# One step of a hybrid decoder on one core: x read by quarters of its rows and transposed on VectorE, with w_in read in the order that this gives

## The chip, the core and the metric

The kernel runs on one core of a Trainium2 chip. Its engines are TensorE (PE in the profile; its weight loads are PEld), VectorE (DVE), ScalarE (ACT), GpSimd (POOL) and SyncE (SP); the last mostly issues transfers, which 16 DMA engines carry out. The metric is the device time of one execution in microseconds (us). Three runs of the kernel before took 2526.93, 2530.73 and 2531.6 us; their median, 2530.73 us, is the time before. The time of the changed kernel is the median of its runs.

## What is computed

One decoder layer for two groups with the same weights: a prompt of 256 tokens and 8 samples of 4 tokens, so 288 tokens of width 2048. All values are 32-bit floats.

```python
def _layer(x, mem_k, mem_v, ssd_conv, ssd_state, gla_state, ffn_conv, p):
    xn = _rmsnorm(x, p['norm_mix'])
    z, xbc, dt_raw, q, k, v, r, g_lr, gate_a, gate_b = _split(xn @ p['w_in'], IN_SIZES)
...
    merged = sigmoid(gate_a) * branch_a + sigmoid(gate_b) * branch_b
    h = x + merged @ p['w_mix_out']
    h = h + _cross_attend(_rmsnorm(h, p['norm_cross']), mem_k, mem_v, p['w_cq'], p['w_co'])
...
```

Ahead of it stand the keys and values of the memory for the prompt, `mn @ w_ck` and `mn @ w_cv` with mn the normalised memory (256 rows). w_in is 2048 x 15408. The sum over the 2048 elements of a token in `xn @ w_in` may be taken in any order, if x and w_in are read in the same one. That freedom is what the change uses.

## The kernel before, in words

**Layout.** Activations stand transposed: features on the 128 partitions, 16 k-tiles of 128 features, and the 288 tokens along the free axis. A projection (`proj`, L158, and `proj_w`, L132) loads a block of four k-tiles by 256 columns of a weight (512 KB, tile `raw`, three buffers) over SP's queue. `wsplit` (L100) cuts each pair of k-tiles into a rounded high part `whi` (ACT, L103) and the rest `wlo` (DVE, L105), five buffers each. TensorE then takes three products per k-tile and 128 columns: high weight by high and by low activation (L147, L148), and low weight by high activation (L151). The next weight block is issued on SP when `wlo` has read the buffer that it takes.

**The first stage.** `mem_proj` (L293) makes the memory's keys and values, eight heads' worth, each in 16 k-steps of six matmuls with 512 columns (L315, L316, L319). It reads w_ck and w_cv by 256 KB per k-step. The first of the eight also prepares the memory rows (tile `mt`, two times 128 rows of 2048 elements). Between the k-steps of the next four, two generators are woven in by `weave` (L172): `x_norm` into heads two and three (L474), `x_prep` into heads four and five (L475).

**x_norm** (L385) loads x by nine transfers of 256 KB over SP's queue: `x_load(0)` brings the 32 sample tokens into `xs`, the other eight a quarter of the columns of 128 prompt rows each into `xp`, which takes the buffer of `mt`. Tokens are on partitions. ACT squares 512 columns at a time with a running sum (L391, twelve instructions, since the 32 sample tokens take four of their own), DVE adds the sums up, ACT takes Ln and Exp of a 128 x 3 tile, which gives each token's 1/rms. Three DVE instructions (L428) put these on diagonals, one TensorE product with ones (L431) spreads them to all partitions, and DVE copies the result to `rtok` (L432).

**x_prep** (L436) runs over the 16 k-tiles. For each, TensorE transposes three 128 x 128 blocks into PSUM (L442, tile `mm`, three buffers), ACT copies the 128 x 288 result to `xf` (L445), every second time SP stores `xf` to the DRAM tensor `x_d` (L447), DVE multiplies the PSUM tile by `rtok` (L449), and `split_from` (L183) multiplies by the gain `norm_mix` and cuts into the high part (ACT, L184) and the low part (DVE, L185). These are the two halves `X(k)` of the activations of every w_in product. The gain comes from `vcol`, a transposed table of the small vectors (`names`, L88).

**Later.** w_in is read by `proj` for all its parts but dt and the gate ranks, which `dt_load` (L486) reads in 32 and 16 columns. `load_x` (L1317) reads `x_d` back over POOL's queue, two k-tiles a transfer, three transfers ahead, for the residual sum at L1337.

**Order.** A scheduler with a model of the engines orders the instructions of each engine when the program is built. The first head of `mem_proj` is ordered by hand, and the nine loads of x keep their order among each other.

Of the kernel before, what the change touches and what calls it, by code (L numbers as in the profile page):

```python
# [8 lines left out]
F32 = mybir.dt.float32  # L9
# [7 lines left out]
P = 128  # L17
D = 2048
# [24 lines left out]
def hybrid_step(ctx: ExitStack, tc: tile.TileContext, I: dict, O: list):  # L43
# [38 lines left out]
    for q in (2, 3):  # L82
# [2 lines left out]

    vcol = const.tile([P, 116], F32, name="vcol")
    scw = const.tile([P, 96], F32, name="scw")
    names = [("norm_mem", 16), ("norm_mix", 16), ("ssd_norm", 16), ("norm_cross", 16), ("norm_ffn", 16),  # L88
             ("b_gla_gate", 8), ("gla_norm", 4), ("ssd_conv_b", 24)]
    vofs = {}  # L90
    dcol = const.tile([P, KT], F32, name="dcol")
# [3 lines left out]
    def vec(name):  # L95
        o, n = vofs[name]
        return vcol[:, o:o + n]
# [34 lines left out]
    def proj_w(load, ncol, X, nk, cons, N=T):  # L132
# [126 lines left out]
    ma_d = dram.tile([P, KT, T], F32, name="ma_d")  # L259
    mg_d = dram.tile([P, KT, T], F32, name="mg_d")  # L260
    ga_d = dram.tile([P, KT // 2, T], F32, name="ga_d")
    x_d = dram.tile([P, KT, T], F32, name="x_d")
    h_d = dram.tile([P, KT, T], F32, name="h_d")

    X = halves(bigr, "xn")
    with pool("p0") as p0:
# [7 lines left out]
        mt = p0.tile([P, 2, D], F32, tag="rows", name="mt")  # L274

        def mem_load(k0):
            cs = slice(k0 * P, (k0 + 2) * P)
# [81 lines left out]
        xts = [xp[:, 0, :], xp[:, 1, :], xs]  # L359
# [15 lines left out]

        def x_load(n):

            if n == 0:
                d = nc.sync.dma_start(out=xs[0:NS], in_=I["x_sample"].rearrange("b l d -> (b l) d"))
            else:  # L380
                i, cs = (n - 1) // 4, slice((n - 1) % 4 * 512, (n - 1) % 4 * 512 + 512)
                d = nc.sync.dma_start(out=xp[:, i, cs], in_=I["x_prompt"][0, i * P:(i + 1) * P, cs])
            tc.keep_in_program_order(d)

        def x_norm():  # L385
            sp4 = p0.tile([P, 3, 4], F32, name="sp4")
            ss = p0.tile([P, 3], F32, name="ss")

            def square(i, q):
                junk = p0.tile([P, 512], F32, name="junk")  # L390
                S.activation(junk, xts[i][:, q * 512:(q + 1) * 512], ACT.Square, accum_out=sp4[:, i, q:q + 1])  # L391

            for step in range(23):
                if step % 2 and step < 18:
                    x_load(step // 2)
                if step == 3:

                    V.tensor_reduce(mrs, mss, AX.X, ALU.add)
                    S.activation(mrs, mrs, ACT.Ln, scale=1.0 / D, bias=epsc[:, 0:1])
                    S.activation(mrs, mrs, ACT.Exp, scale=-0.5)  # L400
                if step == 6:
                    held.pop()()
                if step > 6 and step % 2 == 0 and step < 15:
                    square(2, step // 2 - 4)
                if step > 6 and step % 2:
                    square((step - 7) // 8, (step - 7) // 2 % 4)
# [24 lines left out]
            MM(a[:, 0:T], ones, dg.rearrange("p c t -> p (c t)")[:, 0:T], start=True, stop=True)  # L431
            V.tensor_copy(rtok, a[:, 0:T])  # L432

        rtok = p0.tile([P, T], F32, name="rtok")

        def x_prep():  # L436

            gx = vec("norm_mix")
            for k in range(KT):
                a = mm_tile()  # L440
                for i, xt in enumerate(xts):
                    TR(a[:, i * P:(i + 1) * P], xt[:, k * P:(k + 1) * P], ident)  # L442
                if k % 2 == 0:
                    xf = p0.tile([P, 2, T], F32, tag="xf", bufs=3, name="xf")
                S.copy(xf[:, k % 2, :], a[:, 0:T])  # L445
# [3 lines left out]
                V.tensor_tensor(xr, a[:, 0:T], rtok, ALU.mult)  # L449
# [36 lines left out]
        def dt_load(k0, kn):  # L486
            raw = wp.tile([P, kn, 112], F32, tag="raw", bufs=RB, name="raw")
            for o, c0, n in ((0, O_DT, 32), (32, O_G, 16)):
                nc.sync.dma_start(out=raw[:, :, o:o + n],
                                  in_=I["w_in"][k0 * P:(k0 + kn) * P, c0:c0 + n].rearrange("(k p) n -> p k n", p=P))  # L490
# [1324 lines left out]
```

## Time and profile before

| what | value |
|---|---|
| median of three runs | 2530.73 us (2526.93 to 2531.6) |
| the profiled execution | 2530.86 us, its span 2529.1 us |
| busy, share of the span | PE 99%, PEld 96%, DVE 69%, ACT 53%, POOL 16% |
| moved | 521.96 MB, mean 206 GB/s |
| w_in | 240 loads of 512 KB, and eight small ones |

The profile shows one execution, times in microseconds from the start of its span. A group of instructions is named by its line, engine, operation and the tiles that it writes and reads; "x" is the count, and the last numbers are busy time and the mean of one in nanoseconds. Idle time stands with what ended it ("<-"). In the table by stretches of time each engine has its busy time, then come TensorE's granted clock as a share of full speed, the busy share of the 16 DMA engines and the rate moved.

A matmul's duration in the profile runs from its start through the pipeline, and successive ones overlap. What one takes of TensorE's time is read from the starts of two neighbours, not from its duration.

### The profile page before, as it was taken

Reading aid. Unit: us, or ns where it says so; the run is one execution under the profiler, and the core shown is the slowest. Engines: PE = TensorE matmul, PEld = TensorE weight load, DVE = VectorE, ACT = ScalarE, POOL = GpSimd, SP = SyncE. Lnnn points to the kernel's source line nnn. Section 1 sums busy time; section 2 is a strip of 40 time slices with the busy share of each in tenths; the row PEclk is TensorE's granted clock in tenths of the full one; section 3 lists DMA queues with packets and bytes.
Section 4 is the critical chain, followed back from the end, with each engine's and each line's share of the span. In section 5 each row is a group of like instructions: output and inputs, shape, how many; then the busy total and the mean of one; then the engine's idle time right before and its main releaser. Section 6 shows DMA issues by size and latency. Waiting matters only on the chain.

```text
span 2529.1 us, 50509 instructions
## 1 busy us (share of the span) xinstructions
PE 2508.4 (99%) x18962; PEld 2418.5 (96%) x18962; DVE 1747.9 (69%) x3744; ACT 1342.7 (53%) x2724; POOL 392.2 (16%) x729
## 2 busy tenths in 40 slices
PE   9999999999999999999999999999999999999998
PEld 8889999998999999999999998999999999999998
DVE  6656777786867656667666577667777677675765
ACT  7655647655463645454454554555555455454545
POOL 3002133342300000000001022402111001020010
PEclk9999999999999999999999999999999999999999
DMA  8766587767868676767777699655555555555553
GB/s 268 220 218 196 169 252 206 229 197 209 236 188 271 184 241 185 242 202 265 205 223 249 199 327 322 211 164 173 169 173 170 170 172 172 167 172 171 169 170 130
DMA packets 442022, 521.96 MB, mean 206 GB/s; under 512 B 26876, under 2 KB 390236, under 8 KB 441712
## 3 DMA queue, kind: packets, MB, share of 16 engines
q1 hardware_dynamic: 407728, 422.34, 54.3%
q0 software_dynamic: 34016, 96.38, 12.0%
q8 instruction: 149, 2.44, 0.4%
q14 instruction: 97, 0.79, 0.1%
q10 hardware_dynamic: 32, 0.01, 0.0%
HBM read 473.13 MB, written 45.48 MB: 205 GB/s over the span
## 4 chain that ended last, share of the span: by engine, by line
PE 96%; DMA 2%; DVE 1%; POOL 1%; ACT 0%; issue 0%; DVEq 0%; ACTq 0%
PE acc L148 27%; PE acc L147 27%; PE acc L151 27%; PE acc L315 2%; PE acc L316 2%; PE acc L319 2%; DMA sqr<-in_state_ssd_dram 1%; PE la L1526 1%; PE la L1468 1%; PE mm L1147 1%; PE la L1138 1%; PE mm L1111 1%; POOL sqr L727 0%; DMA raw<-in_w_gla_out_dram 0%; DMA raw<-in_w_in_dram 0%
## 5 line engine op out<-in xcount | busy, mean ns | idle before, releaser
L103 ACT CAST whi<-raw 128x512 fp32r<-128x512 f32 x1464 | 895.1, 618 | 1016.0 <-PE acc L148 753.2
L105 DVE TENSOR_TENSOR wlo<-raw,whi 128x512 fp32r<-128x512 f32 x1464 | 994.4, 686 | 621.5 <-ACT whi L103 607.9
L147 PE MATMUL acc<-xn,whi 128*128 128x288 f32 (+1 forms) x1936 | 550.5, 299 | 0.0
L148 PE MATMUL acc<-xn,whi 128*128 128x288 f32 (+1 forms) x1936 | 542.3, 296 | 0.0
L151 PE MATMUL acc<-xn,wlo 128*128 128x288 f32 (+1 forms) x1936 | 414.1, 295 | 0.0
L148 PE MATMUL acc<-hf,whi 128*128 128x288 f32 x1408 | 393.2, 295 | 0.0
L147 PE MATMUL acc<-hf,whi 128*128 128x288 f32 x1408 | 389.0, 292 | 0.0
L147 PEld LDWEIGHTS acc<-xn,whi 128*128 128x128 f32 (+1 forms) x1936 | 364.7, 188 | 9.8 <-issue 8.1
L148 PEld LDWEIGHTS acc<-xn,whi 128*128 128x128 f32 (+1 forms) x1936 | 365.0, 189 | 6.8 <-issue 4.9
L151 PEld LDWEIGHTS acc<-xn,wlo 128*128 128x128 f32 (+1 forms) x1936 | 310.5, 188 | 1.3 <-issue 1.1
L151 PE MATMUL acc<-hf,wlo 128*128 128x288 f32 x1408 | 294.5, 290 | 0.0
L148 PEld LDWEIGHTS acc<-hf,whi 128*128 128x128 f32 x1408 | 264.5, 188 | 0.1
L147 PEld LDWEIGHTS acc<-hf,whi 128*128 128x128 f32 x1408 | 264.0, 188 | 0.1
L151 PEld LDWEIGHTS acc<-hf,wlo 128*128 128x128 f32 x1408 | 226.1, 188 | 0.0
L148 PE MATMUL acc<-pr,whi 128*128 128x288 f32 x704 | 196.5, 295 | 0.0
L147 PE MATMUL acc<-pr,whi 128*128 128x288 f32 x704 | 195.0, 293 | 0.0
L147 PE MATMUL acc<-un,whi 128*128 128x288 f32 x512 | 145.8, 300 | 2.2 <-ACT whi L103 1.1
L151 PE MATMUL acc<-pr,wlo 128*128 128x288 f32 x704 | 147.4, 290 | 0.0
L148 PE MATMUL acc<-un,whi 128*128 128x288 f32 x512 | 142.9, 295 | 0.0
L1639 POOL COPY fsp<-fst 128x16 f32<-128x16 f32 x88 | 36.6, 419 | 656.5 <-DVE av L1651 422.0
L148 PEld LDWEIGHTS acc<-pr,whi 128*128 128x128 f32 x704 | 132.3, 188 | 0.0
L147 PEld LDWEIGHTS acc<-pr,whi 128*128 128x128 f32 x704 | 132.0, 188 | 0.0
(512 smaller groups left out, 4286.4 us busy)
## 6 DMA issues: line engine op xcount, KB each, us to landing
raw<-in_w_in_dram SPq DMA_DIRECT2D x240, 512.0 KB
raw<-in_w_up_dram SPq DMA_DIRECT2D x176, 512.0 KB
raw<-in_w_down_dram SPq DMA_DIRECT2D x88, 512.0 KB
raw<-in_w_cv_dram SPq DMA_DIRECT2D x32, 512.0 KB
raw<-in_w_ssd_out_dram SPq DMA_DIRECT2D x32, 512.0 KB
sin<-in_state_gla_dram POOLq DMA_DIRECT2D x32, 512.0 KB, 5.8
out_dram<-sin SPq DMA_DIRECT2D x32, 512.0 KB
raw<-in_w_gla_out_dram SPq DMA_DIRECT2D x32, 512.0 KB
```

What stands on the lines that cost most here:

```text
L103: S.copy(hi, raw)
L105: V.tensor_tensor(lo, raw, hi, ALU.subtract)
L147: MM(a, hi[:, k, cs], xh, start=(k0 + s0 + k == 0), stop=False)
L148: MM(a, hi[:, k, cs], xl, start=False, stop=False)
L151: MM(a, lo[:, k, cs], xh, start=False, stop=(k0 + s0 + k == nk - 1))
L315: MM(accs[m], mn_hi[:, kk, ms_], hi[:, 0, :], start=(kk == 0), stop=False)
L316: MM(accs[m], mn_lo[:, kk, ms_], hi[:, 0, :], start=False, stop=False)
L319: MM(accs[m], mn_hi[:, kk, ms_], lo[:, 0, :], start=False, stop=(kk == KT - 1))
L1111: MM(a, kt[:, i, k * P:(k + 1) * P], vt[i], start=True, stop=True)
L1138: MM(osa[NS * j:NS * j + NS, :], qdm[:, k, b, :], sins[b][:, k, :], start=False, stop=(q == 1 and k == 0))
L1147: MM(a, kb[:, k * P:(k + 1) * P], vst, start=True, stop=True)
L1639: G.tensor_copy(sp[:, :, 0:2], st.rearrange("p (b k) -> p b k", k=2))
```

## The change

x is read into one tile `xrow` of nine blocks of 32 tokens. A block has quarter i of the 2048 columns (512 elements) of its 32 tokens on partitions 32i to 32i+31. A DVE transpose turns each 32 x 32 piece with a column step of 16: element 16p+k of a token comes to partition p of k-tile k in the tile `xT`, for 32 tokens an instruction. TensorE's transposes of x and ACT's copies of them are gone. The sample tokens are a block like the others, and the squares become nine instructions of full width.

Since the partitions now hold another choice of features, w_in is read by rows 16p+k (`rows_of`), and the gain `norm_mix` is loaded in this order by a transfer of its own. The copy of x for the residual goes from `xT` to `x_d`, which is now laid out by feature, in four transfers; `load_x` reads it back in the old order of features. The 1/rms takes Ln and Exp after it has been spread to all partitions.

```diff
+    def rows_of(w, row0, k0, kn, c0, ncol):
+        if w is I["w_in"]:
+            return w.rearrange("(p k) n -> p k n", k=KT)[:, k0:k0 + kn, c0:c0 + ncol]
+        return w[row0 + k0 * P:row0 + (k0 + kn) * P, c0:c0 + ncol].rearrange("(k p) n -> p k n", p=P)
...
-            return wload(w[row0 + k0 * P:row0 + (k0 + kn) * P, c0:c0 + ncol].rearrange("(k p) n -> p k n", p=P))
+            return wload(rows_of(w, row0, k0, kn, c0, ncol))
...
-    x_d = dram.tile([P, KT, T], F32, name="x_d")
+    x_d = dram.tile([D, T], F32, name="x_d")
...
-        xp = p0.tile([P, 2, D], F32, tag="rows", name="xp")
-        xs = p0.tile([P, D], F32, name="xs")
-        G.memset(xs, 0.0)
+        xrow = p0.tile([P, 9, 512], F32, tag="rows", name="xrow")
+        xT = p0.tile([P, KT, T], F32, name="xT")
+        gmix = p0.tile([P, KT], F32, name="gmix")
+        G.dma_start(out=gmix, in_=I["norm_mix"].rearrange("(p k) -> p k", k=KT))
...
         def x_load(n):
-            if n == 0:
-                d = nc.sync.dma_start(out=xs[0:NS], in_=I["x_sample"].rearrange("b l d -> (b l) d"))
-            else:
-                i, cs = (n - 1) // 4, slice((n - 1) % 4 * 512, (n - 1) % 4 * 512 + 512)
-                d = nc.sync.dma_start(out=xp[:, i, cs], in_=I["x_prompt"][0, i * P:(i + 1) * P, cs])
-            tc.keep_in_program_order(d)
+            b = n - 1 if n else 8
+            src = I["x_prompt"][0, 32 * b:32 * b + 32] if n else I["x_sample"].rearrange("b l d -> (b l) d")
+            tc.keep_in_program_order(nc.sync.dma_start(out=xrow[:, b, :], in_=src.rearrange("t (i d) -> i t d", i=4)))
...
-            def square(i, q):
+            def square(b):
                 junk = p0.tile([P, 512], F32, name="junk")
-                S.activation(junk, xts[i][:, q * 512:(q + 1) * 512], ACT.Square, accum_out=sp4[:, i, q:q + 1])
+                S.activation(junk, xrow[:, b, :], ACT.Square, accum_out=ss[:, b:b + 1])
+                V.transpose(xT[:, :, 32 * b:32 * b + 32], xrow[:, b, :].rearrange("p (x j) -> p j x", j=KT))
...
-            V.tensor_reduce(ss, sp4, AX.X, ALU.add)
-            S.activation(ss, ss, ACT.Ln, scale=1.0 / D, bias=epsc[:, 0:1])
-            S.activation(ss, ss, ACT.Exp, scale=-0.5)
...
-            dg = p0.tile([P, 3, P], F32, name="dg")
-            for i in range(3):
-                V.tensor_scalar(dg[:, i, :], ident, ss[:, i:i + 1], None, ALU.mult)
+            dg = p0.tile([P, 9, NS], F32, name="dg")
+            V.tensor_tensor(dg, fold4.unsqueeze(1).to_broadcast([P, 9, NS]), ss.unsqueeze(2).to_broadcast([P, 9, NS]), ALU.mult)
...
-            V.tensor_copy(rtok, a[:, 0:T])
+            S.activation(rtok, a[:, 0:T], ACT.Ln, scale=1.0 / D, bias=epsc[:, 0:1])
+            S.activation(rtok, rtok, ACT.Exp, scale=-0.5)
...
             for k in range(KT):
-                a = mm_tile()
-                for i, xt in enumerate(xts):
-                    TR(a[:, i * P:(i + 1) * P], xt[:, k * P:(k + 1) * P], ident)
-                if k % 2 == 0:
-                    xf = p0.tile([P, 2, T], F32, tag="xf", bufs=3, name="xf")
-                S.copy(xf[:, k % 2, :], a[:, 0:T])
-                if k % 2:
-                    nc.sync.dma_start(out=x_d[:, k - 1:k + 1, :], in_=xf)
+                if k % 4 == 0:
+                    nc.sync.dma_start(out=x_d.rearrange("(p k) t -> p k t", k=KT)[:, k:k + 4, :], in_=xT[:, k:k + 4, :])
                 xr = p0.tile([P, T], F32, tag="xr", bufs=3, name="xr")
-                V.tensor_tensor(xr, a[:, 0:T], rtok, ALU.mult)
-                split_from(*X(k), xr, gx[:, k:k + 1])
+                V.tensor_tensor(xr, xT[:, k, :], rtok, ALU.mult)
+                split_from(*X(k), xr, gmix[:, k:k + 1])
...
-        G.dma_start(out=m, in_=x_d[:, 2 * j2:2 * j2 + 2, :])
+        G.dma_start(out=m, in_=x_d[256 * j2:256 * j2 + 256].rearrange("(t p) n -> p t n", p=P))
```

More of the change, by code (lines that the diff above doesn't have):

```diff
@@ L87, in hybrid_step @@
     scw = const.tile([P, 96], F32, name="scw")
-    names = [("norm_mem", 16), ("norm_mix", 16), ("ssd_norm", 16), ("norm_cross", 16), ("norm_ffn", 16),
+    names = [("norm_mem", 16), ("ssd_norm", 16), ("norm_cross", 16), ("norm_ffn", 16),
              ("b_gla_gate", 8), ("gla_norm", 4), ("ssd_conv_b", 24)]
@@ L273, in hybrid_step @@
         S.copy(epsc[:, 2:3], epsc[:, 0:1])
-        mt = p0.tile([P, 2, D], F32, tag="rows", name="mt")
+        mt = p0.tile([P, 9, 512], F32, tag="rows", name="mt")[:, 0:8].rearrange("p (i q) d -> p i (q d)", i=2)
         def mem_load(k0):
@@ L376, in x_load @@
         def x_load(n):
-            if n == 0:
-                d = nc.sync.dma_start(out=xs[0:NS], in_=I["x_sample"].rearrange("b l d -> (b l) d"))
-            else:
-                i, cs = (n - 1) // 4, slice((n - 1) % 4 * 512, (n - 1) % 4 * 512 + 512)
-                d = nc.sync.dma_start(out=xp[:, i, cs], in_=I["x_prompt"][0, i * P:(i + 1) * P, cs])
-            tc.keep_in_program_order(d)
+            b = n - 1 if n else 8
+            src = I["x_prompt"][0, 32 * b:32 * b + 32] if n else I["x_sample"].rearrange("b l d -> (b l) d")
+            tc.keep_in_program_order(nc.sync.dma_start(out=xrow[:, b, :], in_=src.rearrange("t (i d) -> i t d", i=4)))
         def x_norm():
-            sp4 = p0.tile([P, 3, 4], F32, name="sp4")
-            ss = p0.tile([P, 3], F32, name="ss")
-            def square(i, q):
+            ss = p0.tile([P, 9], F32, name="ss")
+            def square(b):
                 junk = p0.tile([P, 512], F32, name="junk")
-                S.activation(junk, xts[i][:, q * 512:(q + 1) * 512], ACT.Square, accum_out=sp4[:, i, q:q + 1])
+                S.activation(junk, xrow[:, b, :], ACT.Square, accum_out=ss[:, b:b + 1])
+                V.transpose(xT[:, :, 32 * b:32 * b + 32], xrow[:, b, :].rearrange("p (x j) -> p j x", j=KT))
             for step in range(23):
@@ L402, in x_norm @@
                     held.pop()()
-                if step > 6 and step % 2 == 0 and step < 15:
-                    square(2, step // 2 - 4)
+                if step == 8:
+                    square(8)
                 if step > 6 and step % 2:
-                    square((step - 7) // 8, (step - 7) // 2 % 4)
+                    square((step - 7) // 2)
                 yield
-            V.tensor_reduce(ss, sp4, AX.X, ALU.add)
-            S.activation(ss, ss, ACT.Ln, scale=1.0 / D, bias=epsc[:, 0:1])
-            S.activation(ss, ss, ACT.Exp, scale=-0.5)
             yield
@@ L424, in x_norm @@
             yield
-            dg = p0.tile([P, 3, P], F32, name="dg")
-            for i in range(3):
-                V.tensor_scalar(dg[:, i, :], ident, ss[:, i:i + 1], None, ALU.mult)
+            dg = p0.tile([P, 9, NS], F32, name="dg")
+            V.tensor_tensor(dg, fold4.unsqueeze(1).to_broadcast([P, 9, NS]), ss.unsqueeze(2).to_broadcast([P, 9, NS]), ALU.mult)
             yield
             a = mm_tile()
-            MM(a[:, 0:T], ones, dg.rearrange("p c t -> p (c t)")[:, 0:T], start=True, stop=True)
-            V.tensor_copy(rtok, a[:, 0:T])
+            MM(a[:, 0:T], ones, dg.rearrange("p c t -> p (c t)"), start=True, stop=True)
+            S.activation(rtok, a[:, 0:T], ACT.Ln, scale=1.0 / D, bias=epsc[:, 0:1])
+            S.activation(rtok, rtok, ACT.Exp, scale=-0.5)
         rtok = p0.tile([P, T], F32, name="rtok")
         def x_prep():
-            gx = vec("norm_mix")
             for k in range(KT):
-                a = mm_tile()
-                for i, xt in enumerate(xts):
-                    TR(a[:, i * P:(i + 1) * P], xt[:, k * P:(k + 1) * P], ident)
-                if k % 2 == 0:
-                    xf = p0.tile([P, 2, T], F32, tag="xf", bufs=3, name="xf")
-                S.copy(xf[:, k % 2, :], a[:, 0:T])
-                if k % 2:
-                    nc.sync.dma_start(out=x_d[:, k - 1:k + 1, :], in_=xf)
+                if k % 4 == 0:
+                    nc.sync.dma_start(out=x_d.rearrange("(p k) t -> p k t", k=KT)[:, k:k + 4, :], in_=xT[:, k:k + 4, :])
                 xr = p0.tile([P, T], F32, tag="xr", bufs=3, name="xr")
-                V.tensor_tensor(xr, a[:, 0:T], rtok, ALU.mult)
-                split_from(*X(k), xr, gx[:, k:k + 1])
+                V.tensor_tensor(xr, xT[:, k, :], rtok, ALU.mult)
+                split_from(*X(k), xr, gmix[:, k:k + 1])
                 yield
@@ L489, in dt_load @@
                 nc.sync.dma_start(out=raw[:, :, o:o + n],
-                                  in_=I["w_in"][k0 * P:(k0 + kn) * P, c0:c0 + n].rearrange("(k p) n -> p k n", p=P))
+                                  in_=rows_of(I["w_in"], 0, k0, kn, c0, n))
             for k in range(kn):
```

1 line of the change is left out of this document (removed).

## The prediction

> **What bounds the kernel now.** I read the page first, for who is busy, then the chain of waits, then the tables by stretches of time, and last TensorE's instructions one by one around x_prep.
>
> ```profile
> span 2529.1 us, 50509 instructions
> PE 2508.4 (99%) x18962; PEld 2418.5 (96%) x18962; DVE 1747.9 (69%) x3744; ACT 1342.7 (53%) x2724; POOL 392.2 (16%) x729
> PE 96%; DMA 2%; DVE 1%; POOL 1%; ACT 0%; issue 0%; DVEq 0%; ACTq 0%
> ```
>
> TensorE sets the end: 96% of the chain that ended last is its work, and it is idle for 2529.1 - 2508.4 = 20.7 us in all. Time goes down if work is taken from TensorE, or if one of its few gaps closes; it goes up if loads come late. So next come the stretches, with two parts of the first stage and the places where transfers are dense.
>
> ```profile
> core 0: us, PE busy (x) PEld busy (x) DVE busy (x) ACT busy (x) POOL busy (x), PEclk, DMA share, GB/s
> 34.00:60.00 26.00, 26.00 (x117) 21.52 (x116) 12.60 (x21) 20.91 (x49) 0.78 (x1) 1.00 0.87 304
> 79.00:122.00 43.00, 43.00 (x213) 35.20 (x213) 31.75 (x61) 31.28 (x64) 2.85 (x10) 1.00 0.72 227
> 240.00:300.00 60.00, 60.00 (x457) 59.52 (x456) 42.19 (x85) 37.97 (x88) 6.45 (x21) 1.00 0.59 176
> 300.00:360.00 60.00, 60.00 (x482) 59.33 (x481) 47.13 (x99) 28.12 (x53) 28.80 (x47) 1.00 0.91 253
> 420.00:480.00 60.00, 60.00 (x483) 59.17 (x483) 45.89 (x99) 31.53 (x67) 29.90 (x51) 1.00 0.87 247
> 540.00:600.00 60.00, 54.51 (x408) 53.32 (x407) 47.14 (x108) 22.67 (x45) 31.67 (x51) 0.94 0.88 248
> 1700.00:2100.00 400.00, 400.00 (x3079) 400.00 (x3078) 295.43 (x715) 214.58 (x469) 51.39 (x108) 1.00 0.56 170
> ```
>
> In the stretches from 34 and from 79 us, where x is squared and then transposed, TensorE is busy all the time, although the DMA engines are 87% busy in the first. So whatever TensorE does there for x is time of the kernel. The one wide gap lies between 540 and 600 us: 60 - 54.51 = 5.5 us, and the clock falls to 0.94 after it.
>
> **The change part by part: TensorE.** The 48 transposes go. Their durations mislead, since a transpose overlaps its neighbours; the starts count.
>
> ```profile
> L442 PE MATMUL mm<-ident,xp x32: 270/272/273, 80.4 to 120.1; 128*128 128x128 f32 x32
> L442 PE MATMUL mm<-ident,xs x16: 272/272/273, 80.6 to 120.2; 128*128 128x128 f32 x16
> ...
> 80.35:121.70 41.35, 21.80 (x52) 10.00 (x53) 1.00 0.73 232
> ```
>
> ```profile
> 45.88 0.39 PE L315 MATMUL acc<-whi,mn_hi 128*128 128x512 f32 x1
> 47.24 0.39 PE L315 MATMUL acc<-whi,mn_hi 128*128 128x512 f32 x1
> ...
> 80.41 0.38 PE L442 MATMUL mm<-ident,xp 128*128 128x128 f32 x2
> ...
> 82.13 0.39 PE L315 MATMUL acc<-whi,mn_hi 128*128 128x512 f32 x1
> ...
> 83.50 0.38 PE L442 MATMUL mm<-ident,xp 128*128 128x128 f32 x2
> ...
> 120.01 0.38 PE L442 MATMUL mm<-ident,xp 128*128 128x128 f32 x2
> ...
> 121.73 0.39 PE L315 MATMUL acc<-whi,mn_hi 128*128 128x512 f32 x1
> ```
>
> A k-step of mem_proj without anything else takes 47.24 - 45.88 = 1.36 us. One with three transposes ahead of it takes 82.13 - 80.41 = 1.72, the plain one after it 83.50 - 82.13 = 1.37. From one step to another that is 0.35 us for three, 16 x 0.35 = 5.6 us. From the whole: 80.41 to 121.73 is 41.32 us, and holds 52 / 2 = 26 k-steps (two L315 each); at 1.36 they would take 35.36, so 5.96 us go. I take 5.8 us, between the two.
>
> The Trainium skill, "TensorE: Matmul & The Clock Gate", Part 4: PE-mode transpose, gives about 275 ns for one inside a kernel. The durations of 272 ns agree, but as a price that would make 48 x 0.275 = 13.2 us; by the starts it is 0.12 us each, and the starts decide.
>
> The spreading of 1/rms (L431) stays as it is: the same 288 columns against ones.
>
> **ACT and DVE.** The rows that price what comes and goes:
>
> ```profile
> L445 ACT COPY xf<-mm 128x288 f32<-128x288 f32 x16 | 6.3, 394 | 1.1
> L391 ACT ACTIVATE junk<-xp 128x512 f32<-128x512 f32 x8 | 5.0, 628 | 0.0
> L449 DVE TENSOR_TENSOR xr<-mm,rtok 128x288 f32<-128x288 f32 x16 | 7.2, 451 | 0.0
> L1332 DVE TENSOR_TENSOR sqa<-sqa,sq 128x288 f32<-128x288 f32 x30 | 13.5, 450 | 0.0
> L878 DVE STREAM_TRANSPOSE st<-sqr 128x512 f32<-128x512 f32 x32 | 21.9, 697 | 0.0
> L189 DVE TENSOR_TENSOR vpl<-kvp,vph 128x1024 fp32r<-128x1024 f32 x4 | 4.9, 1223 | 0.4 <-DMA vc<-in_cache_mem_v_dram 0.3
> L219 ACT ACTIVATE rstd<-mm,epsc 128x288 f32<-128x288 f32 x10 | 5.0, 502 | 0.1
> ```
>
> ACT loses 16 copies (6.3 us) and three squares (1.9 us), and gains Ln and Exp over 288 columns at about 0.5 us each (L219). DVE's three diagonals become one instruction, and one load of `norm_mix` on POOL takes the place of another. DVE's multiply costs the same from SBUF (L1332, 0.450) as from PSUM (L449, 0.451). DVE gains nine transposes of 128 x 512. With both sides dense one takes 0.70 us (L878). Here the source has a step of 64 bytes, which no row shows. Lower bound 0.70; upper bound what twice as many elements take, 1.22 us (L189). I take 0.70, as the same operation on the same number of elements: 6.3 us, at most 11 us. DVE is idle for 26 - 12.60 = 13.4 us from 34 to 60, so even 11 fit, and TensorE's work covers all of this. Without that cover each transpose would put 0.70 us ahead of the `wlo` queued behind it, and that `wlo` holds up both TensorE's third product and SP's next weight load. How much cover there is shows in the counts up to 68 us, where it is thinnest, of `wlo` (L105, first row) and of the products that use it (L319, second row, two per k-step):
>
> ```profile
> 0.00:68.00 68.00, 28.01 (x42) 1.00 0.82 266
> ...
> 0.00:68.00 68.00, 25.19 (x82) 1.00 0.82 266
> 67.59 1.14 ACT L103 CAST whi<-raw 128x512 fp32r<-128x512 f32 x2 [4.18 <-DMA raw<-in_w_ck_dram]
> ```
>
> 42 against 82 / 2 = 41: one k-step, 1.36 us, ahead. What was late there was a weight load, 4.18 us, not DVE. A delay of 0.7 us in a `wlo` still fits into that. Zero, then, and up to 2 us lost in the range.
>
> **Transfers.** The nine loads of x move 256 KB each before and after, at the same places on SP; what changes is that the sample block now waits for the buffer of `mt`, whose last reader ends at 31.6 us. Behind it on SP stands a weight load that went out at 32.84 anyway.
>
> ```profile
> 31.38 0.19 ACT L347 ACTIVATION_READ_ACCUMULATOR junk<-mt 128x1 f32 x1
> ...
> 29.11 0.42 SPq L379 DMA_DIRECT2D xs<-in_x_sample_dram  x1
> 32.84 0.37 SPq L114 DMA_DIRECT2D raw<-in_w_cv_dram  x1
> ```
>
> The stores of x become four of 576 KB, and SP's queue no longer holds weight loads behind a wait for `xf`. Reading x_d back in pieces half as long, on POOL's queue, is hidden by its lead of three transfers; only if that lead were gone would the residual sum wait for it. All this at zero.
>
> w_in's 240 loads keep their number, size and runs of 1 KB. Only the places in DRAM change: neighbouring partitions are 16 rows apart (986112 bytes) instead of one (61632), and the four runs of a partition one row apart instead of 128. The trace has loads with the same runs and row steps of 45056 and 8192 bytes, w_up and w_down: 170 / 0.56 = 304 GB/s while busy in the row from 1700 us, against 176 / 0.59 = 298 for w_in in the row from 240. No row has a step near 986112. I take no difference; the other end is a rival.
>
> **Sum.** In the profiled execution: 2530.86 - 5.8 = 2525.1 us (span 2529.1 - 5.8 = 2523.3). The median stands 0.1 us below that execution: 2525 us.
>
> **The rivals.**
>
> *Forecast: the transposes' time is gained whole, 2525.* Its own range is 2522 to 2528.
>
> *The gain is eaten by late transfers, about 2530.* For it: w_in loads that went out at 565.2 reached ACT only at 574.2, and TensorE stood 5.5 us and then had a lower clock.
>
> ```profile
> 565.21 1.58 SPq L114 DMA_DIRECT2D raw<-in_w_in_dram  x2
> ...
> 574.21 1.14 ACT L103 CAST whi<-raw 128x512 fp32r<-128x512 f32 x2 [7.11 <-DMA raw<-in_w_in_dram]
> 575.56 0.80 PE L890 MATMUL mm<-bblk,wst 128*128 128x256 f32 x2 [5.49 <-ACT cst L603]
> ```
>
> A second such gap costs 5.5 us: 2525.1 + 5.5 = 2530.6. Against it: of 2529.1 us only 20.7 are idle, so such gaps are rare. The same place may also fall out well: everything after 122 us comes 5.8 us earlier against POOL's loads, and if the gap closes, 2525 - 5.5 = 2519.5.
>
> *The transposes starve TensorE, 2530 to 2536.* At twice the upper price, 2.4 us, nine ask for 22 us where DVE has 13.4, and the excess of 8 us falls on TensorE: 2533. It decides from 13.4 / 9, 1.5 us each. For it: the one k-step of lead. Against it: no DVE row of this size takes that long.
>
> The Trainium skill, "SBUF — State Buffer", Door 1: The DMA port swizzle, says that accesses that leave a 16-byte line each time pay a penalty; a step of 64 bytes does so at every element. It gives no figure for DVE, and no run here shows it.
>
> *w_in is read more slowly, 2543.* This is the rival on the other side: DRAM serves steps of 986112 bytes worse. TensorE needs 512 KB per 24 products of 400 / 3079 = 0.130 us, 3.12 us, or 168 GB/s. In the stretch from 300 us that is 168 / 253 of a DMA share of 0.91, 0.60. It decides when the share reaches 1, at 0.09 / 0.60, loads 15% slower. A third slower adds 0.20: shares of 1.11, 1.07 and 1.08 in the three stretches of 60 us, 60 x 0.26 = 16 us, and some 2 us at the other dense places: 2525 + 18 = 2543. For it: no load in the trace has such a step. Against it: steps from 8192 to 61632 bytes all reach about 300 GB/s.
>
> The Trainium skill, "DMA: Bandwidth & Descriptors", Latency and other measured facts, is the rule against this change: copies whose partitions were 512 KiB apart ran at 207 GB/s, 2 MiB at 164, 4 MiB at 103, and 4 MiB plus 4 KiB at 214. The step here, 963 KiB, lies between the first two; as a plain rule on distance the loads would take up to 207 / 164, a quarter more, and an estimate from the shares above gives 1.06, 1.02 and 1.03, so 60 x 0.11 = 7 us and about 2532; that case is part of this rival's chance. By its last figure, it is powers of two that are slow, and 963 KiB is none; then nothing changes. No run here shows either.
>
> **How the numbers follow.** What a measurement of this kernel can tell from no change is 0.2%, 5.06 us, so the bounds are 2525.7 and 2535.8; the forecast lies just beyond the lower one. Chances: forecast 0.44 (of it 0.36 faster, 0.08 within), gap closed 0.10 (faster), gain eaten 0.22 (within), transposes starve 0.04 (half within, half slower), w_in slower 0.20 (slower). Faster 0.46, same 0.32, slower 0.22. The range goes from 2516, beyond the closed gap by what its lower clock cost (0.20 of 15 us, 3 us), to 2542, which leaves out half of the w_in rival.
>
> ```profile
> 565.00:580.00 15.00, 9.51 (x57) 9.24 (x57) 10.71 (x27) 3.06 (x6) 7.89 (x12) 0.80 0.98 281
> ```
>
> **What would show it.** Right: from 34 us to the first w_in product TensorE is busy throughout, every k-step takes 1.36 us, and that product starts 5.8 us before 127.8; the nine transposes take about 0.70 us; a w_up stretch and a w_in stretch show the same GB/s per DMA share as before. Wrong: idle TensorE between 34 and 122 with `wlo` named; transposes above 1.5 us; waits of `whi` for w_in far above the 61.6 us of before, or shares at 1 between 300 and 600.
>
> ```profile
> 127.83 0.29 PE L147 MATMUL acc<-xn,whi 128*112 128x288 f32 x1
> ...
> ACT whi L103 <- DMA raw<-in_w_in_dram: 61.6, 30, 7.1
> ```

## The result: 2538.36 us, and the profile after

The changed kernel takes 2538.36 us (median of 6 runs, 2537.51 to 2542.11), the kernel before 2529.19 us (6 runs, 2526.19 to 2531.6). The medians differ by 9.2 us; the measured ratio is 1.0045, 95% interval 1.0035 to 1.0056, which is 8.9 to 14.2 us slower, where 5.8 us of gain were forecast. The profiled execution took 2538.35 us, against 2530.86 before. First its page:

```profile
span 2536.6 us, 50366 instructions
PE 2506.0 (99%) x18914; PEld 2413.2 (95%) x18914; DVE 1755.2 (69%) x3749; ACT 1337.8 (53%) x2702; POOL 390.2 (15%) x728
PE 93%; DMA 3%; DVE 1%; issue 1%; POOL 1%; ACT 0%; SPq 0%; DVEq 0%; ACTq 0%
```

TensorE's work fell, from 2508.4 to 2506.0 us, and its idle time rose from 20.7 to 2536.6 - 2506.0 = 30.6 us. Its share of the chain that ended last fell from 96% to 93%. The rest of the chain grew at the transfers, of which `xrow` alone has 1% of the span. Where the idle time lies shows in the table by stretches, columns as before. Here are two rows of the kernel before that the prediction did not show, and then the kernel after:

```profile
34.00:127.83 93.83, 93.83 (x441) 77.15 (x440) 57.66 (x106) 63.87 (x135) 5.76 (x18) 1.00 0.75 243
...
60.00:79.00 19.00, 19.00 (x85) 15.70 (x84) 10.48 (x20) 9.99 (x20) 0.73 (x1) 1.00 0.78 248
```

```profile
core 0: us, PE busy (x) PEld busy (x) DVE busy (x) ACT busy (x) POOL busy (x), PEclk, DMA share, GB/s
34.00:60.00 26.00, 20.19 (x77) 14.88 (x76) 12.35 (x17) 11.30 (x26) 0.78 (x1) 0.91 0.60 201
60.00:79.00 19.00, 16.17 (x65) 12.29 (x64) 12.75 (x19) 11.45 (x24) 0.73 (x1) 0.95 0.70 244
79.00:122.00 43.00, 39.47 (x176) 31.95 (x175) 32.04 (x63) 26.11 (x49) 1.43 (x2) 1.00 0.76 251
240.00:300.00 60.00, 60.00 (x457) 59.52 (x457) 43.51 (x86) 37.84 (x87) 6.37 (x19) 1.00 0.61 178
300.00:360.00 60.00, 60.00 (x484) 59.33 (x483) 46.71 (x97) 30.17 (x62) 29.23 (x51) 1.00 0.83 234
540.00:600.00 60.00, 57.66 (x450) 56.15 (x450) 50.11 (x114) 25.43 (x53) 31.21 (x50) 0.97 0.87 248
...
34.00:140.08 106.08, 93.91 (x393) 74.07 (x392) 65.16 (x111) 56.20 (x113) 6.24 (x20) 0.97 0.67 217
```

The first w_in product (the end of the last row) starts at 140.08 us instead of 127.83, 12.25 us later, and TensorE is idle for nearly as long: 106.08 - 93.91 = 12.17 us, where the kernel before had none. (TensorE's busy time in this row isn't lower than before, although 48 transposes are gone: the clock is 0.97, and up to 34 us it had done 31.45 us of work instead of 32.87, since it waited 1.4 us for the memory rows there. The runs a3 and a4 below, with the same loads, did 32.81 and 32.87 us up to there, so that wait comes from the execution and not from the change.) After this product the changed kernel needs 2536.6 - 140.08 = 2396.5 us against 2529.1 - 127.83 = 2401.3. Of these 4.8 us it gains 57.66 - 54.51 = 3.1 at the old gap between 540 and 600. Together 12.25 - 4.75 = 7.5 us, the difference of the spans. The first three rows hold 5.81 + 2.83 + 3.53 = 12.2 us of idle time. In the first two the DMA engines are less busy than before (0.60 instead of 0.87, 0.70 instead of 0.78), so there it is not a lack of their total rate.

Who waited for what up to 130 us, in the table of waits (waiter, line, releaser; total us, times, longest):

```profile
ACT junk L393 <- DMA xrow<-in_x_prompt_dram: 15.2, 8, 3.0
DVE xT L394 <- DMA xrow<-in_x_prompt_dram: 13.7, 8, 3.2
...
PE acc L325 <- DVE wlo L105: 7.7, 6, 2.3
...
PE acc L321 <- ACT whi L103: 4.5, 3, 2.8
```

Every one of the eight prompt blocks kept ACT and DVE waiting, 15.2 and 13.7 us in all. How this comes to TensorE shows in the timeline (start, duration, engine, line, operation; idle time before it and what ended it), here SP's queue, DVE and TensorE:

```profile
31.95 0.75 SPq L386 DMA_DIRECT2D xrow<-in_x_sample_dram  x1
33.62 0.59 SPq L386 DMA_DIRECT2D xrow<-in_x_prompt_dram  x1
...
38.44 1.03 DVE L394 STREAM_TRANSPOSE xT<-xrow 128x512 f32<-128x512 f32 x1 [4.07 <-DMA xrow<-in_x_sample_dram]
39.39 1.25 DVE L105 TENSOR_TENSOR wlo<-raw,whi 128x512 fp32r<-128x512 f32 x2
40.10 0.72 PE L325 MATMUL acc<-wlo,mn_hi 128*128 128x512 f32 x2 [2.31 <-DVE wlo L105]
43.84 1.06 DVE L394 STREAM_TRANSPOSE xT<-xrow 128x512 f32<-128x512 f32 x1 [3.20 <-DMA xrow<-in_x_prompt_dram]
44.83 0.65 DVE L105 TENSOR_TENSOR wlo<-raw,whi 128x512 fp32r<-128x512 f32 x1
45.53 0.73 PE L325 MATMUL acc<-wlo,mn_hi 128*128 128x512 f32 x2 [1.17 <-DVE wlo L105]
...
75.05 3.13 SPq L440 DMA_DIRECT2D x_d<-xT  x4
78.28 2.54 SPq L114 DMA_DIRECT2D raw<-in_w_ck_dram  x2
87.00 0.50 PE L321 MATMUL acc<-whi,mn_hi 128*128 128x512 f32 x1 [2.81 <-ACT whi L103]
```

The block issued at 31.95 is there at 38.44, the one issued at 33.62 at 43.84: 6.5 and 10.2 us. Before, a block of the same size was used 4.6 us after its issue (33.3 to 37.9), and no square waited at all. On DVE the transpose that waits for x stands ahead of a `wlo` whose weights are there: this `wlo` starts, without a wait of its own, when the transpose is through (38.44 plus 1.03, then 39.39), and TensorE's third product waits for it. The last three rows show a second loss: the four stores of x leave in a row, take 3.13 us of SP's queue, the weight loads stand behind them, and at 87.00 TensorE has waited 2.81 us for `whi`. Here the DMA engines are full: their share is 0.95 to 1.04 in each of the stretches 76 to 79, 79 to 82, 82 to 84 and 84 to 87 us. So the 2.36 MB of the stores count there, besides the time on SP's queue.

Why x is late shows in a stretch where loads of x are nearly all that is under way:

```profile
44.20:46.60 2.40, 1.23 (x6) 0.89 (x6) 1.87 (x3) 2.12 (x6) 0.00 (x0) 0.84 0.26 102
```

The DMA share is 0.26 and the rate 102 GB/s: about four of the 16 engines work, the others have nothing to do. The source of the load is `"t (i d) -> i t d"` with i = 4 as its outermost dimension. The Trainium skill, "DMA: Bandwidth & Descriptors", "Why a DMA increments its semaphore by 16 and not by 1", says that a transfer goes to as many engines as the largest number up to 16 that divides the slowest dimension on both sides; its "Rules for kernel authors" say so again. By that four carry this load, and the share of 0.26 agrees.

### The profile page after: what moved, and what is told of

Its sections match the earlier page's. It is cut to its first block, busy times and chain, and to the rows that moved or that the text cites. A ratio compares the mean times of both kernels' runs of the same rounds, so it can differ in the third digit from the quotient of the medians.

```text
span 2536.6 us, 50366 instructions
## 1 busy us (share of the span) xinstructions
PE 2506.0 (99%) x18914; PEld 2413.2 (95%) x18914; DVE 1755.2 (69%) x3749; ACT 1337.8 (53%) x2702; POOL 390.2 (15%) x728
## 4 chain that ended last, share of the span: by engine, by line
PE 93%; DMA 3%; DVE 1%; issue 1%; POOL 1%; ACT 0%; SPq 0%; DVEq 0%; ACTq 0%
PE acc L148 27%; PE acc L147 27%; PE acc L151 26%; PE acc L321 2%; PE acc L325 2%; PE acc L322 2%; DMA xrow<-in_x_prompt_dram 1%; DMA sqr<-in_state_ssd_dram 1%; PE la L1519 1%; PE mm L1140 1%; PE la L1131 1%; PE la L1461 1%; PE mm L1104 1%; DMA raw<-in_w_gla_out_dram 0%; POOL sqr L720 0%
```

## The experiments

The theory: the form of the load puts x on four engines, its lateness stops ACT and DVE, and the bunched stores add a gap; the transposes' gain is real but covered. The rivals: w_in's order, the slower transposes on DVE, the order or length of the rows read, SP's issue time. Medians in us, with the ratio to the kernel before in the same shared runs (2529.11 for a1 to a4, 2528.53 for b1, a5, a6 and c1, 2528.2 for d1 to d5; 29 runs each):

| run | edit | median (runs) | ratio, 95% |
|---|---|---|---|
| a3_win_old | after, w_in in the old order | 2538.79 (6) | 1.0042 [1.0028, 1.0057] |
| a4_dense_turn | after, transposes read densely | 2538.39 (8) | 1.0037 [1.0023, 1.0051] |
| b1_before_quarters | before, with the load form of after | 2539.21 (4) | 1.0043 [1.0026, 1.0059] |
| a2_token_first | after, tokens outermost in the load | 2527.92 (10) | 0.9996 [0.9984, 1.0008] |
| a1_four_loads | after, each load in four of 64 KB | 2532.39 (12) | 1.0013 [1.0003, 1.0024] |
| a6_spread_only | after, stores held apart | 2534.38 (10) | 1.0023 [1.0012, 1.0033] |
| a5_token_first_spread | a2 and a6 | 2522.78 (12) | 0.9981 [0.9971, 0.9992] |
| c1_sixteen_spread | 32 partitions by four blocks a load, stores apart | 2532.92 (12) | 1.0012 [1.0, 1.0023] |
| d5_halves | a6, two outermost | 2556.17 (4) | 1.0107 [1.0086, 1.0127] |
| d4_eighths | a6, eight outermost | 2522.55 (10) | 0.9981 [0.9969, 0.9994] |
| d1_four_spread | a1 and a6 | 2524.31 (12) | 0.9984 [0.9972, 0.9996] |
| d3_two_queues | d1, half of the loads from POOL | 2524.23 (12) | 0.9989 [0.9975, 1.0002] |

b1, a2, a3, a4, a5, d4 and d5 combine other elements than the layer asks for (d5 also leaves out the sample tokens) and serve only to measure. The other five compute the layer.

**Two rivals: w_in's order (a3) and the transposes (a4).**

```diff
-        if w is I["w_in"]:
-            return w.rearrange("(p k) n -> p k n", k=KT)[:, k0:k0 + kn, c0:c0 + ncol]
```

> The changed kernel with w_in read in the old order of rows; the products then sum wrong pairs, the output is not the reference's. Theory W: 5 us or more faster than the changed kernel, and the stretches from 185 to 1190 us show more GB/s per DMA share. Theories F and T: 2536 to 2541, as the changed kernel, and idle TensorE between 34 and 122 us stays at 10 to 14 us.

```diff
-                V.transpose(xT[...], xrow[:, b, :].rearrange("p (x j) -> p j x", j=KT))
+                V.transpose(xT[...], xrow[:, b, :].rearrange("p (j x) -> p j x", j=KT))
```

> The changed kernel with the transposes of x reading dense 32 x 32 pieces (other elements, so the output is not the reference's). All theories: one takes 0.70 us in place of 1.06. Theory T: the idle time of TensorE between 34 and 122 us falls by more than half and the time to 2532 or less. Theories F and W: at most 1 us faster, 2536 to 2541.

Without the new order of w_in the time is 2538.79 us, with it 2538.36: no cost of it shows. Nine dense transposes change nothing either (2538.39), although they are a third shorter, as the view of tile `xT` shows, first in the changed kernel and then in a4 (shortest, median and longest in ns, first and last start):

```profile
L394 DVE STREAM_TRANSPOSE xT<-xrow x9: 1033/1059/1083, 38.4 to 74.0; 128x512 f32<-128x512 f32 x9
```

```profile
L394 DVE STREAM_TRANSPOSE xT<-xrow x9: 711/711/712, 37.9 to 73.0; 128x512 f32<-128x512 f32 x9
```

The step of 64 bytes costs 1.06 - 0.71 = 0.35 us each, 3.1 us of DVE in all, and these fall into time in which DVE waits for x anyway. Both rivals fall. What dense transposes would bring where x comes in time was not tried.

**The form of the load alone: put into the kernel before (b1), taken out of the one after (a2).**

```diff
-                d = nc.sync.dma_start(out=xp[:, i, cs], in_=I["x_prompt"][0, i * P:(i + 1) * P, cs])
+                d = nc.sync.dma_start(out=xp[:, i, cs],
+                    in_=I["x_prompt"][0, 32 * (n - 1):32 * n].rearrange("t (i d) -> i t d", i=4))
```

> The kernel before with only the source of the eight loads of the prompt's x in the changed kernel's form, 32 tokens with the quarter as the slowest dimension, 4; x is permuted, the output is not the reference's. Theory F (4 of 16 DMA engines): x lands 6 us and more after its issue, ACT waits for xp in the squares, TensorE stands idle between 34 and 122 us for 8 us or more where it had no idle time, and the time is 2536 to 2545. Rival (x is late in the changed kernel for another reason, as its buffer or the transposes): 2527 to 2531 and no idle time.

```diff
-            ... in_=src.rearrange("t (i d) -> i t d", i=4)
+            ... in_=src.rearrange("t (i d) -> t i d", i=4)
```

> The changed kernel with the token ahead of the quarter in the source of each load of x: one load, same bytes, same runs of 2 KB, but the slowest dimension is 32 in place of 4. A piece goes to partition 4t+i instead of 32i+t, so x is permuted and the output is not the reference's; every instruction is the same. Theory F: x lands within 5 us of its issue instead of 6 to 13, and the time is that of the kernel with four loads, 2525 to 2529. Theories T and W: as the changed kernel, 2536 to 2540.

The kernel before loses 2539.21 - 2528.53 = 10.7 us by the form of these eight loads, with all its transposes, squares and stores as they were. The changed kernel gains 2538.36 - 2527.92 = 10.4 us by the other order of the same bytes. In b1 TensorE is idle where it was in the changed kernel, and its first w_in product starts at 140.01 us. No transpose stands on DVE there: it is the squares on ACT that wait for x and hold up the `whi` behind them, and the seven waits for `whi`, in the last row, are the 106.01 - 97.16 = 8.8 us of idle time:

```profile
34.00:60.00 26.00, 20.82 (x81) 15.50 (x79) 7.80 (x12) 13.76 (x33) 0.78 (x1) 0.93 0.67 216
60.00:79.00 19.00, 15.33 (x63) 11.70 (x64) 8.61 (x16) 10.23 (x22) 0.73 (x1) 1.00 0.59 191
...
34.00:140.01 106.01, 97.16 (x437) 77.01 (x436) 57.56 (x105) 63.15 (x134) 6.42 (x20) 0.98 0.68 214
...
PE acc L315 <- ACT whi L103: 8.8, 7, 2.6
```

In a2 TensorE is busy from 34 to 60 us again, with the DMA share at 0.90 and 298 GB/s. What is left is one gap after the four stores, which start between 60.9 and 62.7 us there. The stretches:

```profile
34.00:60.00 26.00, 26.00 (x115) 21.03 (x114) 18.88 (x27) 16.17 (x36) 0.78 (x1) 1.00 0.90 298
60.00:79.00 19.00, 16.11 (x62) 12.68 (x61) 16.53 (x35) 12.40 (x26) 0.73 (x1) 0.82 0.85 294
```

The gap in TensorE's timeline:

```profile
72.94 0.79 PE L321 MATMUL acc<-whi,mn_hi 128*128 128x512 f32 x1 [2.89 <-ACT whi L103]
```

**The stores (a6, a5).** One edit holds them at their places among the k-tiles of x_prep; a5 has it together with a2.

```diff
-                    nc.sync.dma_start(out=x_d.rearrange("(p k) t -> p k t", k=KT)[:, k:k + 4, :], in_=xT[:, k:k + 4, :])
+                    tc.keep_in_program_order(nc.sync.dma_start(out=x_d.rearrange("(p k) t -> p k t", k=KT)[:, k:k + 4, :], in_=xT[:, k:k + 4, :]))
```

> The changed kernel with only the stores of x_d pinned at their places in x_prep, loads of x as in the changed kernel. Theory S: the gap of 2.8 us at 87 us is gone and the time is 2533 to 2537; the waits for x before 76 us stay. Rival: no change, 2537 to 2540.

> The kernel with the token first in the loads of x, and the four stores of x_d pinned at their places in x_prep, about 7 us apart, in place of four in a row at 61 us. Theory S (the 2.36 MB of stores in a row make the weight loads behind them late): the gap of 2.9 us at 73 us is gone, the stretch from 60 to 122 us has no idle TensorE, 2523 to 2526. Rival (the gap has another cause, as the lead being thin there): the gap stays or moves by a few us, 2527 to 2529.

The edit is worth 2538.36 - 2534.38 = 4.0 us alone and 2527.92 - 2522.78 = 5.1 us with a2. In a6 the stores start from 84.3 to 111.0 us, and TensorE is busy from 79 to 122, while the losses up to 79 us stay:

```profile
34.00:60.00 26.00, 18.89 (x79) 14.01 (x77) 12.53 (x17) 11.05 (x23) 0.78 (x1) 1.00 0.66 214
60.00:79.00 19.00, 14.75 (x61) 10.99 (x61) 12.95 (x21) 10.96 (x24) 0.73 (x1) 1.00 0.62 199
79.00:122.00 43.00, 43.00 (x194) 35.29 (x193) 31.02 (x62) 26.45 (x51) 1.43 (x2) 1.00 0.83 274
```

With both, a5 is faster than the kernel before, and shows what the transposes were worth on TensorE:

```profile
34.00:124.36 90.36, 89.14 (x390) 71.92 (x389) 63.28 (x110) 54.14 (x111) 6.31 (x18) 1.00 0.79 252
```

From 34 us to the first w_in product TensorE works 89.14 us at full clock instead of 93.83: 4.7 us are gone. 90.36 - 89.14 = 1.2 us of idle time are left, with transposes of 1.07 us each.

**Is it the number of engines, or the rows? (d5, d4.)** Both theories make i-first loads slow, one by the number of engines, the other by the order or the length of the rows. So the outermost dimension was made two and eight, with the stores held apart.

```diff
+            c, h = (0, 0) if n == 0 else divmod(n - 1, 2)
+            src = I["x_prompt"][0, 64 * c:64 * c + 64, 1024 * h:1024 * h + 1024]
-            ... in_=src.rearrange("t (i d) -> i t d", i=4)
+            ... in_=src.rearrange("t (i d) -> i t d", i=2)
```

> x loaded by halves, 256 KB a transfer with the half slowest (2 by 64 rows by 512 elements, runs of 2 KB as in the changed kernel), stores held at their places. The elements land elsewhere and the sample tokens are not read, so the output isn't the reference's. If the slowest dimension sets the number of engines, two carry it: a DMA share of 0.13 at some 51 GB/s while only a load of x is under way, 5.1 us for 256 KB alone, and a time well above a6_spread_only's 2534.4: 2545 to 2565. If rows or their order cost, it is as a6: 2532 to 2536.

```diff
+            for r in range(2):
+                ... out=xrow[:, b, 256 * r:256 * r + 256],
+                    in_=src[16 * r:16 * r + 16].rearrange("t (i d) -> i t d", i=8)
```

> x loaded by eighths of its rows, two transfers of 128 KB a block with the eighth slowest (8 by 16 rows by 256 elements), stores held at their places. The elements land elsewhere, so the output isn't the reference's. If the number of DMA engines of a load is the largest number up to 16 that divides its slowest dimension, eight carry it: while only a load of x is under way the DMA share is 0.5 at some 205 GB/s (0.26 at 102 in the changed kernel), and the time lies near that of a5_token_first_spread: 2523 to 2528. If it is the order or the length of the rows read that costs (runs of 1 KB now, half as long), 2534 as in a6_spread_only, or more.

With two outermost the kernel takes 2556.17 us, 21.8 more than a6 with four. With eight it takes 2522.55, the same as a5 with 32, though the rows it reads are half as long (1 KB). The stretches of d5: one in which little but x is loaded, and then the three of the stage:

```profile
46.60:47.80 1.20, 0.00 (x0) 0.00 (x0) 0.67 (x1) 0.67 (x2) 0.00 (x0) 1.00 0.13 51
...
34.00:60.00 26.00, 17.43 (x50) 12.56 (x49) 7.86 (x11) 6.63 (x14) 0.78 (x1) 0.74 0.44 149
60.00:79.00 19.00, 12.91 (x42) 8.93 (x40) 6.42 (x8) 5.58 (x12) 0.00 (x0) 0.82 0.38 132
79.00:122.00 43.00, 35.51 (x137) 28.09 (x138) 30.89 (x60) 25.64 (x52) 1.45 (x2) 0.88 0.60 200
```

A share of 0.13 at 51 GB/s is two engines of 16, half of the 0.26 at 102 above: some 25 GB/s an engine either way. In d4 the share is about half, 0.55, in a stretch that a load of x nearly fills:

```profile
45.10:46.40 1.30, 0.92 (x4) 0.78 (x5) 1.30 (x3) 1.14 (x2) 0.00 (x0) 1.00 0.55 185
```

Times of 2556, 2534, 2523 and 2523 us for 2, 4, 8 and 32 outermost: this is the number of engines, as the Trainium skill's rule has it, and the rows' order and length don't show. From eight on no cost shows here any more.

**Ways around it (a1, c1).** The elements have to land by quarters on the partitions, so a whole block can't be loaded with its tokens outermost. a1 cuts each load into the four quarters, and in each the 32 tokens are outermost. c1 loads one quarter of four blocks (256 KB on 32 partitions) at a time, with the stores held apart and the squares and transposes moved to when such a group is complete.

```diff
+            for i in range(4):
+                ... out=xrow[32 * i:32 * i + 32, b, :], in_=src[:, 512 * i:512 * i + 512]
```

> The changed kernel with each load of x cut into four, one for each quarter of the columns (32 partitions, 64 KB). Theory F (few DMA engines): a load whose source has the quarter as its slowest dimension, 4, is served by only 4 of the 16 DMA engines; x and the weight loads that share those engines land late. With 32 as the slowest dimension the idle time of TensorE between 34 and 122 us (12.3 us in the changed kernel) falls below 3 us, the periods of about 4 us between the landings of x are gone, and the time is 2525 to 2530. Theory T (the transposes, 1.06 us each with the strided source, delay wlo): the idle time stays above 8 us, 2535 to 2539. Theory W (w_in in its new order is slower): 2535 to 2539 as well.

```diff
+            h, i = divmod(n - (n > 4), 4)
+                ... out=xrow[32 * i:32 * i + 32, 4 * h:4 * h + 4, :],
+                    in_=I["x_prompt"][0, 128 * h:128 * h + 128, 512 * i:512 * i + 512].rearrange("(b t) d -> t b d", t=32)
...
+                for b in {13: [0], 15: [1], 17: [2], 18: [8], 19: [3], 21: [4, 5], 22: [6, 7]}.get(step, []):
+                    square(b)
```

> A version meant to beat both: the loads of x by quarter of the columns and half of the prompt (32 partitions, four blocks of 32 tokens each, 256 KB, slowest dimension 32), the sample tokens in four small ones, squares and transposes moved behind the last quarter of each half, and the stores of x_d pinned. Theories F and S: no idle TensorE between 34 and 122 us, 2522 to 2526, 3 to 7 us faster than before. Rival (transposes and squares of the second half come in a heap and delay wlo): a gap of 1 to 3 us between 60 and 80 us, 2526 to 2530.

Both missed. Their traces are of long executions among their twelve (2536.52 us for a1, the slowest, and 2539.09 for c1). a1 has its largest gap, 4.37 us at 79.87, after the four stores, which left from 66.3 us on. c1 has other gaps, and DVE's timeline shows the first of the two large ones:

```profile
47.66 3.92 DVE L401 STREAM_TRANSPOSE xT<-xrow 128x512 f32<-128x512 f32 x4
51.50 1.26 DVE L105 TENSOR_TENSOR wlo<-raw,whi 128x512 fp32r<-128x512 f32 x2
...
52.21 0.73 PE L325 MATMUL acc<-wlo,mn_hi 128*128 128x512 f32 x2 [2.64 <-DVE wlo L105]
...
70.32 0.73 PE L325 MATMUL acc<-wlo,mn_hi 128*128 128x512 f32 x2 [2.82 <-DVE wlo L105]
```

Blocks that become ready together are transposed together: four in a row take 3.92 us of DVE, and the `wlo` behind them comes 2.64 us late. Here the transposes do starve TensorE, in heaps, which they don't one at a time. (Ahead of the second heap DVE also waited 1.87 us for x.)

**The version to keep (d1), and SP's issue time (d3).** d1 is a1 with the stores held apart; d3 issues quarters 1 and 3 of each block from POOL.

> Each load of x cut in four of 32 partitions (64 KB), as in a1_four_loads, and the four stores of x held at their places in x_prep. If the 4.37 us gap of a1 at 79.87 us came from the burst of stores alone, it goes: 2532.4 - 4.4 = 2528, the same as before (2526 to 2530). If 36 issues on SP at 0.45 to 0.8 us each are what makes weight loads late, the gaps of about 1 us at 46, 53 and 67 us stay and grow: 2530 to 2533.

```diff
+                q = nc.sync if i % 2 == 0 else nc.gpsimd
+                tc.keep_in_program_order(q.dma_start(out=xrow[32 * i:32 * i + 32, b, :], in_=src[:, 512 * i:512 * i + 512]))
```

> As d1_four_spread, with two of the four loads of each block issued on POOL's queue instead of SP's. If SP's issue time is what is left, 2522 to 2526 and faster than before. If POOL's queue is late with them, because vectors and masks stand ahead of them there, the first squares wait: gaps between 34 and 60 us with DVE wlo or ACT whi named, 2528 to 2535.

d1 takes 2524.31 us, faster than the kernel before by 0.16% (0.9984, 0.9972 to 0.9996) and than the changed one by 14 us. The 8.1 us from a1 to d1 are more than a1's one gap, and more than was expected; why was not followed up. TensorE is idle 92.57 - 89.48 = 3.1 us up to the first w_in product:

```profile
34.00:60.00 26.00, 24.36 (x106) 19.05 (x104) 16.79 (x23) 13.93 (x30) 0.78 (x1) 1.00 0.90 268
60.00:79.00 19.00, 17.55 (x75) 13.36 (x74) 15.17 (x28) 14.03 (x29) 0.73 (x1) 1.00 0.77 237
79.00:122.00 43.00, 43.00 (x192) 35.36 (x191) 30.24 (x57) 25.26 (x47) 2.19 (x6) 1.00 0.82 259
...
34.00:126.57 92.57, 89.48 (x390) 71.52 (x389) 63.39 (x110) 54.57 (x109) 5.69 (x18) 1.00 0.81 246
```

Taking half of the 36 issues off SP changes nothing (2524.23), so no cost of SP's issue time shows. d3's upper bound is 1.0002, so that it is faster than the kernel before isn't shown.

## Why the prediction was wrong, point by point

- **What bounds the kernel: right.** TensorE sets the end before and after, and each gap of it is time of the kernel.
- **TensorE's gain of 5.8 us: real, sized 1.1 us too high.** Where x comes in time (a5), 4.7 us of TensorE's work are gone up to the first w_in product, and the kernel is 1 - 0.9981 = 0.19% faster (0.08 to 0.29%), 2.0 to 7.3 us. Why the starts of the k-steps gave 5.6 to 5.96 stays open. Part of it may be six other transposes (tile `srow`): before they stand in two groups of three (0.8 us of TensorE's busy time), in a5 one by one (1.3 us).
- **ACT and DVE: hidden, as forecast.** The transposes took 1.06 us, between the bounds of 0.70 and 1.22, not the 0.70 taken; in the changed kernel a4 shows no cost of this, and in a5, where x comes in time, TensorE waits for `wlo` for 0.3 us in all. The point from which they would starve TensorE, 1.5 us each, was not reached and so not tested. It was reckoned for transposes spread out: c1's heaps starve TensorE at 0.98 us each.
- **"The nine loads of x move 256 KB each before and after, at the same places on SP ... All this at zero": this step failed.** Bytes, count and places were counted, not the order of the dimensions: the load went from 128 partitions outermost to four. b1 gives it 10.7 us, a2 10.4. The quoted row on cover was read too narrowly with it: one k-step of lead, 1.36 us, was compared with a slower `wlo` (0.7 us), not with a block of x for which DVE waits up to 3 to 4 us ahead of that `wlo`. The rule on it (the Trainium skill, as above), which speaks against this change, was not weighed.
- **"The stores of x become four of 576 KB ... at zero": failed too, 4.0 to 5.1 us** (a6, a5). That SP's queue no longer holds weight loads behind a wait for `xf` was counted as nothing lost. But before, the eight stores went out from 84.5 to 121.0 us, each behind its `xf`; without that wait the scheduler put four in a row, from 75.0 to 76.9, ahead of the weight loads. That the wait had spread them is read from these two orders; what the row costs is measured.
- **w_in's order: right, at zero.** The 300 us stretch moves 234 / 0.83 = 282 GB/s while busy, against 253 / 0.91 = 278 before, and a3 without the order takes the same time within what these runs can tell. The plain rule on distance that the prediction drew from the Trainium skill, "DMA: Bandwidth & Descriptors", "Latency and other measured facts", is not borne out at 963 KiB.
- **The rivals.** "The gain is eaten by late transfers, about 2530" had the kind of cause right, but put it at w_in after 500 us and priced it at one gap of 5.5 us. It was x's own loads and the bunched stores, 12.2 us of idle time. The gap after 500 us became smaller: 5.49 us before, 2.34 after. The case with 2519.5 had this in part, but not by its mechanism, an earlier start: the gap is 2.15 us in a5, which comes there earlier, 2.37 in a6, and still 5.40 in b1, the kernel before with late x. So it belongs to the change and not to the shift; which part of the change closes it was not tried.
- **The range.** The measured time lies inside it, and that is luck: above 2536 the range stands there for w_in alone, which costs nothing that shows, and no rival had the loads of x or the order of the stores.
- **What would show it.** The row named as sign of a wrong prediction, idle TensorE between 34 and 122 us with `wlo` named, is the one that came; transposes above 1.5 us, named beside it, did not.

In the changed kernel the parts add up, step by step through the medians: 2522.78 - 2528.53 = -5.8 us for what is gained with x in time and the stores apart (a5), +5.1 for the stores in a row (a2), +10.4 for the form of the loads, together +9.8 us, against 9.2 between the medians and 8.9 to 14.2 by the ratio. The loads' 10.7 us in b1 and the stores' 4.0 in a6 check two of these from the other side.

## What to carry to other kernels

A transfer's cost isn't its bytes: look at the outermost dimension of both sides, and where it is small (two and four cost time here, eight did not) count how many DMA engines are left; in the trace a DMA share that stays at k/16 while one load is under way gives it away. Price a late operand by what stands behind its waiting instruction on an engine that works in order, here the weights of another product. When a change removes a wait, ask what that wait had kept apart, and hold stores at their places if loads for the bottleneck share their queue and the DMA engines.

## What the runs showed of the hardware

- One DMA engine moved some 25 GB/s: 51 GB/s at a share of 0.13 with two outermost, 102 at 0.26 with four.
- Stretches with loads onto 32 partitions moved fewer bytes for the same share: from 34 to 60 us a2 had 298 GB/s at 0.90, d1 268 at 0.90, and c1 244 at 0.91, as the row below shows. What limits them wasn't tried.

```profile
34.00:60.00 26.00, 21.68 (x92) 16.52 (x91) 13.60 (x19) 12.08 (x27) 0.78 (x1) 1.00 0.91 244
```

- DVE's transpose of 128 x 512 takes 0.71 us from a dense source and 1.06 us from one with a step of 64 bytes. The Trainium skill, "SBUF — State Buffer", Door 1: The DMA port swizzle, has a penalty for accesses that leave a 16-byte line each time, without a figure for DVE; a4 agrees that there is one.
